# Gate and up products of two token chunks in seven block products for eight, with the last chunk in a pass of its own

## The chip, the cores and the metric

The kernel runs on one core of one Trainium2 chip. The metric is the device time of one execution in microseconds. A core has a matrix engine (TensorE, PE in the rows), VectorE (DVE), ScalarE (ACT), GpSimd (POOL) and SyncE (SP, which here issues all DMAs). Matmuls write to banks in PSUM; tiles lie in SBUF, weights and results in the chip's memory.

## The reference, cut to what matters

One layer of a hybrid encoder: a modulated RMSNorm, one input projection, eight stick-breaking and eight forgetting attention heads, an output projection, and a SwiGLU feed-forward, for 1024 prompt tokens and 64 sample tokens. D_MODEL is 1024, D_FF is 2816, everything is float32. What the change touches:

```python
x = x + (1.0 + ada[2]) * (o @ w_o)
h = rmsnorm(x, g_ffn) * (1.0 + ada[4]) + ada[3]
f = (jax.nn.silu(h @ w_gate) * (h @ w_up)) @ w_down
x = x + (1.0 + ada[5]) * f
y = rmsnorm(x, g_final)
```

## The kernel before, in words

Activations lie transposed, features on the 128 partitions and tokens along the columns. The 1088 tokens form three chunks (`CH`, line 29) of 384, 384 and 320 columns; the last holds 256 prompt tokens and the 64 sample tokens, so each of its modulated steps is two instructions (`pieces`, line 157). D_MODEL is eight tiles of 128 (`KT`), D_FF twenty-two blocks of 128 (`NFF`).

Every dense product keeps float32 accuracy through two parts: an operand is rounded to a high part (`hi`, a ScalarE copy, line 173) and the rest is its low part (`lo`, a subtraction of two SBUF tensors, line 176). A product is then three matmuls per k tile, high by high, low by high and high by low (`dense`, lines 422 to 429).

After attention, `out_block` (line 850) multiplies with `w_o`; `evac_plain` (line 1019) adds to the residual `x1`, `square1` (line 1047) sums the squares, and `norm2(c)` (line 1061) makes the feed-forward's input of chunk c: column sums and a reciprocal root (`token_cols`, `rstd_cols`, lines 187 to 215), spread over all partitions by small matmuls (`spread`, line 217), then a scale (line 1086), a shift with rounding to the high part `h2h` (line 1090) and the low part `h2l` (line 1091) for each of eight tiles.

The feed-forward (lines 1160 to 1228) runs over eleven groups of two D_FF blocks. `load_ff` (line 1165) loads a block's columns of `w_gate` and `w_up`, 512 KB each, and splits them, the low part on VectorE. `hidden` (line 1177) makes, for one block and one chunk, the gate and up products of 24 matmuls each in banks tagged `z`, then silu on ScalarE, the multiply by the up product, the rounding to `dh` and the low part `dl`. Then the group's two `w_down` blocks are loaded and split, and for each chunk and each of eight output tiles m six matmuls are summed in one of three banks (`t`, `t`, `acc`, line 1212) and VectorE adds the result to `x1` (line 1222). In the last group `weigh` (line 1127) also sums squares for the final norm, and `final(c)` (line 1139) transposes chunk c, scales and stores it.

The order of the instructions is a planner's: it takes them by priority and simulated time, per engine, so work whose operands are ready passes work that waits. Each engine then runs its own list strictly in order. Tiles of one tag rotate through a fixed number of buffers, and a DMA into a tile waits for the last reader of the buffer's former tile.

## Time and profile before

| | us |
|---|---|
| median of three runs (1682.41 to 1685.65) | 1683.74 |
| profiled execution | 1681.39 |
| its span, first to last instruction | 1679.2 |
| TensorE busy in the span | 1580.3 (94%) |
| one feed-forward group, 1045.36 to 1116.81 | 71.45 |

How to read the rows below: a stretch of time is given in us from the span's start. Busy time of an engine is the time in which it ran at least one instruction; behind it stands the number of instructions. "[2.24 <-DVE x L1022]" behind an instruction is the engine's idle time before it and the instruction that ended it. A number after L is a line of the kernel. Neighbouring instructions of one engine overlap a little, so starts are better than durations for a pace.

### The profile page before, as it was taken

Reading aid. Unit: us, or ns where it says so; the run is one execution under the profiler, and the core shown is the slowest. Engines: PE = TensorE matmul, PEld = TensorE weight load, DVE = VectorE, ACT = ScalarE, POOL = GpSimd, SP = SyncE. Lnnn points to the kernel's source line nnn. Section 1 sums busy time; section 2 is a strip of 40 time slices with the busy share of each in tenths; the row PEclk is TensorE's granted clock in tenths of the full one; section 3 lists DMA queues with packets and bytes.
Section 4 is the critical chain, followed back from the end, with each engine's and each line's share of the span. In section 5 each row is a group of like instructions: output and inputs, shape, how many; then the busy total and the mean of one; then the engine's idle time right before and its main releaser. Section 6 shows DMA issues by size and latency. Waiting matters only on the chain.

```text
span 1679.2 us, 26182 instructions
## 1 busy us (share of the span) xinstructions
PE 1580.3 (94%) x9822; PEld 1487.7 (89%) x9822; DVE 947.0 (56%) x1828; ACT 657.1 (39%) x1410; POOL 604.9 (36%) x556
## 2 busy tenths in 40 slices
PE   8898998988899977998999999999999999999998
PEld 4697887867888966987989999999999999999997
DVE  5659767598557565676895334334443344334336
ACT  5466656577445553555454021120211112021127
POOL 2558778797668774773360000000000000000004
PEclk9999999999999987999999999999999999999999
DMA  9433333321444552463332021110202102021002
GB/s 309 165 102 93 110 92 100 93 78 32 125 121 121 151 144 63 114 184 100 91 101 63 2 76 39 38 51 26 76 15 62 51 26 71 6 76 50 27 26 107
DMA packets 174750, 141.61 MB, mean 84 GB/s; under 512 B 14336, under 2 KB 167584, under 8 KB 174624
## 3 DMA queue, kind: packets, MB, share of 16 engines
q1 hardware_dynamic: 174624, 139.94, 28.8%
q8 instruction: 78, 1.28, 0.3%
q14 instruction: 48, 0.39, 0.1%
HBM read 105.60 MB, written 27.08 MB: 79 GB/s over the span
## 4 chain that ended last, share of the span: by engine, by line
PE 65%; DVE 4%; POOL 2%; DMA 1%; ACT 1%; issue 1%; SPq 1%; DVEq 0%; POOLq 0%; ACTq 0%
PE gu L428 10%; PE gu L429 10%; PE gu L427 10%; PE acc_d L1219 5%; PE acc_d L1217 5%; PE acc_d L1218 5%; PE acc L427 2%; PE acc L428 2%; PE acc L429 2%; PE ps_av L756 2%; PE pt_a L747 2%; PE acc_o L427 2%; PE acc_o L428 1%; PE acc_o L429 1%; PE ps_z L691 1%
## 5 line engine op out<-in xcount | busy, mean ns | idle before, releaser
L428 PE MATMUL gu<-h,wff_l 128*128 128x384 f32 (+1 forms) x1056 | 345.3, 327 | 0.0
L429 PE MATMUL gu<-h,wff_h 128*128 128x384 f32 (+1 forms) x1056 | 345.1, 327 | 0.0
L427 PE MATMUL gu<-h,wff_h 128*128 128x384 f32 (+1 forms) x1056 | 343.5, 327 | 0.0
L1222 DVE SCALAR_TENSOR_TENSOR x<-acc_d,ada,x 128x384 f32<-128x384 f32 (+1 forms) x352 | 167.0, 498 | 251.2 <-PE acc_d L1219 251.1
L1135 POOL TENSOR_TENSOR sums<-sums,sq 128x384 f32<-128x384 f32 (+1 forms) x17 | 16.8, 990 | 774.7 <-ACT sq L1134 770.8
L427 PE MATMUL acc<-h,whi 128*128 128x384 f32 (+1 forms) x576 | 199.5, 346 | 5.7 <-DVE kraw L500 3.2
L428 PEld LDWEIGHTS gu<-h,wff_l 128*128 128x128 f32 x1056 | 198.2, 188 | 0.0
L429 PEld LDWEIGHTS gu<-h,wff_h 128*128 128x128 f32 x1056 | 198.2, 188 | 0.0
L427 PEld LDWEIGHTS gu<-h,wff_h 128*128 128x128 f32 x1056 | 198.0, 188 | 0.0
L429 PE MATMUL acc<-h,whi 128*128 128x384 f32 (+1 forms) x576 | 193.3, 336 | 3.7 <-DVE h L404 3.7
L428 PE MATMUL acc<-h,wlo 128*128 128x384 f32 (+1 forms) x576 | 193.5, 336 | 0.0
L1217 PE MATMUL acc_d<-dh,wdh 128*128 128x384 f32 (+1 forms) x528 | 173.5, 329 | 0.1
L1219 PE MATMUL acc_d<-dl,wdh 128*128 128x384 f32 (+1 forms) x528 | 172.9, 328 | 0.0
L1218 PE MATMUL acc_d<-dh,wdl 128*128 128x384 f32 (+1 forms) x528 | 172.8, 327 | 0.0
L711 DVE TENSOR_TENSOR_SCAN kp<-kp 128x384 f32<-128x384 f32 (+4 forms) x104 | 140.1, 1354 | 37.5 <-ACT kp L707 35.5
L1184 ACT ACTIVATE sg<-gu 128x384 f32<-128x384 f32 (+1 forms) x66 | 31.3, 474 | 279.2 <-PE gu L429 279.2
L1186 ACT CAST dh<-sg 128x384 fp32r<-128x384 f32 (+1 forms) x66 | 32.5, 493 | 269.6 <-DVE sg L1185 269.6
L747 PE MATMUL pt_a<-ident,a_t 128*128 128x128 f32 x608 | 103.9, 283 | 30.3 <-DVE aT L753 17.0
L441 ACT CAST aT<-pt_a 128x384 fp32r<-128x384 f32 (+3 forms) x208 | 98.9, 481 | 82.0 <-PE pt_a L747 70.7
L753 DVE TENSOR_TENSOR aT<-pt_a,aT 128x384 fp32r<-128x384 f32 (+3 forms) x208 | 110.0, 535 | 36.4 <-ACT aT L441 35.5
L715 POOL TENSOR_TENSOR a_t<-a_t,kp 128x383 f32<-128x383 f32 (+6 forms) x104 | 114.1, 1105 | 31.7 <-DVE kp L711 10.3
L427 PEld LDWEIGHTS acc<-h,whi 128*128 128x128 f32 x576 | 111.4, 193 | 10.9 <-DVE kraw L500 3.6
(307 smaller groups left out, 3334.0 us busy)
## 6 DMA issues: line engine op xcount, KB each, us to landing
lowraw<-in_w_ada SPq DMA_DIRECT2D x32, 512.0 KB, 3.5
wraw<-in_w_in SPq DMA_DIRECT2D x24, 512.0 KB, 6.4
wraw<-in_w_gate SPq DMA_DIRECT2D x22, 512.0 KB
wraw<-in_w_up SPq DMA_DIRECT2D x22, 512.0 KB, 3.7
wraw_d<-in_w_down SPq DMA_DIRECT2D x22, 512.0 KB, 3.5
wa<-in_w_ada SPq DMA_DIRECT2D x16, 512.0 KB, 6.7
oT_d<-ot SPq DMA_DIRECT2D x128, 64.0 KB, 2.1
wraw<-in_w_o SPq DMA_DIRECT2D x14, 512.0 KB, 3.3
```

What stands on the lines that cost most here:

```text
L427: pe.matmul(out=acc, lhsT=wh[:, kt, :], rhs=rh[kt], start=st, stop=False)
L428: pe.matmul(out=acc, lhsT=wl[:, kt, :], rhs=rh[kt], start=False, stop=False)
L429: pe.matmul(out=acc, lhsT=wh[:, kt, :], rhs=rl[kt], start=False, stop=sp_)
L441: act.copy(out=out, in_=in_)
L711: dve.tensor_tensor_scan(out=rev, data0=rev, data1=rev, initial=1.0 if b == w else kp[:, b:b + 1], op0=ALU.mult, op1=ALU.min)
L715: eng[E_AM[qt]].tensor_tensor(out=a_t[:, :wm], in0=a_t[:, :wm], in1=kp[:, a + 1:a + 1 + wm], op=ALU.mult)
L747: pe.transpose(out=pt[:, j * P:(j + 1) * P], in_=at[a][:, j * P:(j + 1) * P], identity=ident)
L753: dve.tensor_tensor(out=tl, in0=pv, in1=f32(th), op=ALU.subtract)
L1217: pe.matmul(out=a_, lhsT=wh[:, m, :], rhs=dh[:, t0:t0 + n], start=(i == 0), stop=False)
L1218: pe.matmul(out=a_, lhsT=wl[:, m, :], rhs=dh[:, t0:t0 + n], start=False, stop=False)
L1219: pe.matmul(out=a_, lhsT=wh[:, m, :], rhs=dl[:, t0:t0 + n], start=False, stop=(i == G - 1))
L1222: dve.scalar_tensor_tensor(out=xc[:, a:b], in0=acc[:, a:b], scalar=ada[:, 5, m, s:s + 1], in1=xc[:, a:b], op0=ALU.mult, op1=ALU.add)
```

## The change

The eight input tiles k of a gate or up product, two D_FF blocks and the first two chunks form two by two blocks each. Seven products of sums of blocks replace the eight block products (Strassen's scheme in Winograd's form). The weight sums (`Seven`) are four GpSimd instructions on 512 columns for each matrix and group, and each of the seven weight operands is split by `prep`, the low part on VectorE. The activation operands are seven sets of four tile pairs, made once by `norm2_steps` in pieces between the work of pass 1. `Blocks` multiplies: twelve matmuls a product, accumulated in three banks, with copies and adds between them.

The last chunk can't be paired, so it gets a pass of its own over all 22 blocks ahead of the others (pass 1, the loop over `f0`), with all weights loaded and split once for it and once more for chunks 0 and 1 (pass 2, the loop over `g0`). In pass 1, three of six low parts of a group are GpSimd's; in pass 2, that of `wd[0]`. The weight tiles rotate through four raw buffers and three pairs of parts. Inside the feed-forward the planner is switched off for TensorE, ScalarE, VectorE and GpSimd (`manual_schedule`): they run in the order of the program. The norms of chunks 0 and 1 (`rms_rows`) come in the first down loop of pass 1. `down_begin` starts three blocks with one of the two D_FF blocks before the other is needed. The final norm of the last chunk moves into the first group of pass 2, that of chunk 1 among the last down blocks; chunk 0 ends the kernel.

The core of the diff; chunk 1 is c = 1, and `later(left)` issues the low parts that were put off:

```diff
-    def norm2(c):
+    def rms_rows(c, out=None):
+
         n = CH[c][1]
...
+        def part_tiles():
+
+            i = count["w"] % 3
+            count["w"] += 1
+            return tuple((wpool if i < 2 else fp).tile([P, KT, P], F32R, tag=t, name=t) for t in ("whi", "wlo"))
...
+        def part(src, hi, lo, lo_eng=dve):
+            act.copy(out=hi, in_=src)
+            lo_eng.tensor_tensor(out=lo, in0=src, in1=f32(hi), op=ALU.subtract)
+            return hi, lo
...
+        def down_begin(wd, dd, c, ahead=1):
+
+            for m in range(3):
+                begun[m] = bank(("t", "t", "acc")[m % 3], "acc_d")
+                down_products(begun[m], wd, dd, c, m, ahead, True)
+
+        def down_block(wd, dd, c, m, last, ahead=1):
+
+            n = CH[c][1]
+            if m in begun:
+                acc = begun.pop(m)
+            else:
+                acc = bank(("t", "t", "acc")[m % 3], "acc_d")
+                down_products(acc, wd, dd, c, m, ahead, True)
+            down_products(acc, wd, dd, c, m, 1 - ahead, False)
...
+            if last:
+                weigh(m, c, xc, n)
...
+                for kt, c, w in ((k, 0, "11"), (k, 1, "12"), (4 + k, 1, "22"), (4 + k, 0, "21")):
+                    def scale(kt=kt, c=c, w=w, b=b):
+                        t = b[w] = opl.tile([P, 384], F32, tag=("xn2", "sq")[c], name=f"n{w}")
+                        dve.scalar_tensor_tensor(
+                            out=t, in0=x1[kt][c], scalar=sc2[:, kt, 0:1], in1=sacc[c], op0=ALU.mult, op1=ALU.mult)
...
+                    def diff(out=out, x_=x_, y_=y_, b=b):
+                        pool.tensor_tensor(out=b[out], in0=b[x_], in1=b[y_], op=ALU.subtract)
...
+                    def low(out=out, k=k, w=w, b=b):
+                        dve.tensor_tensor(out=bh[w, k, 1], in0=b[out], in1=f32(bh[w, k, 0]), op=ALU.subtract)
+                    chains.append((diff, high, low))
...
+            for i in range(len(chains) + 2):
+                yield [chains[i - j][j] for j in (2, 1, 0) if 0 <= i - j < len(chains)]
...
-        G = 2
-        for g0 in range(0, NFF, G):
...
+        def half_tile():
+            if spare:
+                return spare.pop()
+            t = part_tiles()
+            spare.append([x_[:, 4:8] for x_ in t])
+            return [x_[:, 0:4] for x_ in t]
+
+        class Seven:
+
+            def __init__(self, f0, w):
+                r1, r2 = (raw_tile(col_src(w, f0 + i)) for i in range(2))
+                self.a11, self.a12, self.a21, self.a22 = r1[:, 0:4], r1[:, 4:8], r2[:, 0:4], r2[:, 4:8]
+                self.ops = []
+
+            def sums_first(self):
+                self.s1 = fp.tile([P, 4, P], F32, tag="s1", name="s1")
+                pool.tensor_tensor(out=self.s1, in0=self.a21, in1=self.a22, op=ALU.add)
+                pool.tensor_tensor(out=self.a21, in0=self.a11, in1=self.a21, op=ALU.subtract)
+
+            def sum2(self):
+                pool.tensor_tensor(out=self.a11, in0=self.s1, in1=self.a11, op=ALU.subtract)
+
+            def sum4(self):
+                pool.tensor_tensor(out=self.a12, in0=self.a12, in1=self.a11, op=ALU.subtract)
+
+            def prep(self):
+                src = (self.a11, self.a12, self.a11, self.s1, self.a21, self.a12, self.a22)[len(self.ops)]
+                self.ops.append(part(src, *half_tile()))
...
+        BAND = ("11", "21", "T2", "T1", "T3", "22", "T4")
...
+            def product(self, i):
...
+                acc = getattr(self, "zxzvzvz"[i])
+                wh, wl = self.s.ops[i]
+                for k in range(4):
+                    for j, (w_, r_) in enumerate(((wh, 0), (wl, 0), (wh, 1))):
+                        pe.matmul(
+                            out=acc, lhsT=w_[:, k, :], rhs=bh[BAND[i], k, r_],
+                            start=(i in (0, 1, 3) and k == 0 and j == 0),
+                            stop=(k == 3 and j == 2), skip_group_check=True)
+
+            def evac(self, i):
+                if i == 0:
+                    self.m1 = gu_tile("m1")
+                    act.copy(out=self.m1, in_=self.z)
+                elif i == 1:
+                    dve.tensor_tensor(out=self.m1, in0=self.m1, in1=self.x, op=ALU.add)
+                    self.done(0, 0, self.m1, self.m1)
+                elif i == 2:
+                    self.u2 = gu_tile("u2")
+                    act.copy(out=self.u2, in_=self.z)
+                elif i == 3:
+                    self.m5 = gu_tile("m5")
+                    act.copy(out=self.m5, in_=self.v)
+                elif i == 4:
+                    dve.tensor_tensor(out=self.m5, in0=self.m5, in1=self.z, op=ALU.add)
+                    self.done(1, 1, self.m5, self.m5)
+                elif i == 5:
+                    dve.tensor_tensor(out=self.u2, in0=self.u2, in1=self.v, op=ALU.add)
+                    self.done(0, 1, self.u2, self.u2)
+                else:
+                    self.done(1, 0, self.z, None)
+
+        ET = mybir.EngineType
+        in_order = tc.manual_schedule(engines={ET.PE, ET.Activation, ET.DVE, ET.Pool})
...
+        def ready(*key, lo_eng=dve):
+            parts[key] = part(raws.pop(key), *part_tiles(), lo_eng)
...
+        def gated(ff, gu):
+            sg = sgs.pop(ff)
+            dve.tensor_tensor(out=sg, in0=sg, in1=gu[:, :n2], op=ALU.mult)
+            dh, dl = (gu_tile("d", F32R)[:, 0:n2] for _ in range(2))
+            dds[ff % 2, 2] = dh, dl
+            act.copy(out=dh, in_=sg)
+            left.append(lambda: dve.tensor_tensor(out=dl, in0=sg, in1=f32(dh), op=ALU.subtract))
+
+        silu(0, gate_up("g", 0))
+        for g, f0 in enumerate(groups):
+            last = f0 + 2 == NFF
+            f1 = f0 + 1
+
+            gu = gate_up("u", f0)
+            ready("u", f1, lo_eng=pool)
+            fetch("d", f0)
+            gated(f0, gu)
+            gu = gate_up("g", f1)
+            later(left)
+            if g > 0:
+                step2()
+            fetch("d", f1)
+            if last:
...
+            else:
+                fetch("g", f0 + 2)
+                ready("g", f0 + 2)
+            silu(f1, gu)
+            if g > 0:
+                step2()
+            gu = gate_up("u", f1)
+            ready("d", f0, lo_eng=pool)
+            gated(f1, gu)
+            later(left)
...
+            else:
+                gu = gate_up("g", f0 + 2)
+                ready("d", f1)
+                silu(f0 + 2, gu)
+                fetch("u", f0 + 2)
+                fetch("g", f0 + 3)
+            wd = [parts.pop(("d", f0)), parts.pop(("d", f1))]
+            dd = {(i, 2): dds.pop((i, 2)) for i in range(2)}
+            if g > 0:
+                step2()
+            down_begin(wd, dd, 2, 0)
+            for m in range(KT):
+                down_block(wd, dd, 2, m, last, 0)
+                if m == 0 and not last:
+                    ready("u", f0 + 2, lo_eng=pool)
+                if g > 0 and m == 6:
+                    step2()
...
+                if g == 0 and m in (2, 5):
+                    rms_rows(m // 3, sacc[m // 3])
+            if not last:
+                fetch("u", f0 + 3)
+                ready("g", f0 + 3)
...
+        cur7 = first7
+        for gi, g0 in enumerate(groups):
...
+            def up(i, c, src, out):
+                s_ = sg[i, c]
+                dve.tensor_tensor(out=s_, in0=s_, in1=src, op=ALU.mult)
+                dh, dl = (hb.tile([P, 384], F32R, tag="dd", bufs=8, name="d") for _ in range(2))
+                act.copy(out=dh, in_=s_)
+                left.append(lambda: dve.tensor_tensor(out=dl, in0=s_, in1=f32(dh), op=ALU.subtract))
+                dd[i, c] = dh, dl
...
+            else:
+                B = Blocks(cur7, ("z", "z", "z"), gate)
+            for i in range(7):
+                if gi or i > 1:
+                    B.product(i)
+                if i == 0 and gi:
+                    cur7.prep()
+                    cur7.prep()
+                elif i == 1:
+                    cur7.prep()
+                    cur7.prep()
+                    up7 = Seven(g0, w_up)
+                elif i == 2:
+                    cur7.prep()
+                    up7.sums_first()
+                    up7.prep()
+                    up7.sum2()
+                    raws["d", 1] = raw_tile(down_src(g0 + 1))
+                elif i == 4:
+                    up7.prep()
+                    up7.sum4()
+                    up7.prep()
+                    raws["d", 0] = raw_tile(down_src(g0))
+                elif i == 6:
+                    up7.prep()
+                    up7.prep()
+                if gi or i > 0:
+                    B.evac(i)
+            B = Blocks(up7, ("av", "z", "u"), up)
+            for i in range(7):
+                B.product(i)
+                later(left)
...
+                if i == 1:
+                    up7.prep()
+                    up7.prep()
+                    if not last:
+                        nx7 = Seven(g0 + 2, w_gate)
+                elif i == 3:
+                    wd = [None, part(raws.pop(("d", 1)), *part_tiles())]
+                    if not last:
+                        nx7.sums_first()
+                elif i == 5:
+                    wd[0] = part(raws.pop(("d", 0)), *part_tiles(), pool)
+                B.evac(i)
+            down_begin(wd, dd, 1)
+            later(left)
+            for bi, (c, m) in enumerate([(c, m) for c in (1, 0) for m in range(KT)]):
+                down_block(wd, dd, c, m, last)
+                if not last:
+                    if bi in (1, 2):
+                        nx7.prep()
+                    elif bi == 3:
+                        nx7.sum2()
+                        nx7.sum4()
+                elif c == 0 and m == 2:
+                    col1 = final_cols(1)
+                elif c == 0 and m in (4, 5, 6):
+                    final_tile(col1, 1, m - 4)
+                if gi == 0 and c == 1:
+                    if m in (3, 5, 7):
+                        final_last(col2, m // 2 - 1)
+            if not last:
+                cur7 = nx7
+        in_order.__exit__(None, None, None)
+        col0 = final_cols(0)
+        for j in range(3):
+            final_tile(col0, 0, j)
```

## Rows read from the trace of the kernel before

**Rows 1.** Busy time of the engines over the span, the page's first part:
```profile
PE 1580.3 (94%) x9822; PEld 1487.7 (89%) x9822; DVE 947.0 (56%) x1828; ACT 657.1 (39%) x1410; POOL 604.9 (36%) x556
```

**Rows 2.** Stretches: length, busy PE, PEld, DVE, ACT, POOL (instructions), granted clock, DMA share, GB/s:
```profile
845.00:862.00 17.00, 13.99 (x78) 13.25 (x78) 16.50 (x33) 10.00 (x23) 12.66 (x9) 1.00 0.34 105
862.00:876.00 14.00, 14.00 (x82) 14.00 (x81) 11.54 (x19) 7.32 (x14) 9.32 (x7) 0.88 0.27 77
876.00:930.00 54.00, 54.00 (x325) 53.79 (x324) 32.15 (x60) 23.68 (x38) 1.57 (x1) 1.00 0.23 69
...
1188.26:1616.94 428.68, 428.68 (x2593) 428.68 (x2593) 170.90 (x301) 70.93 (x109) 0.00 (x0) 1.00 0.15 45
```

**Rows 3.** Timeline of TensorE in one group: start us, duration us, engine, line, instruction:
```profile
1045.03 0.33 PE L429 MATMUL gu<-h,wff_h 128*128 128x384 f32 x1
...
1057.68 0.31 PE L427 MATMUL gu<-h,wff_h 128*128 128x320 f32 x1
...
1063.84 0.31 PE L427 MATMUL gu<-h,wff_h 128*128 128x320 f32 x1
```

**Rows 4.** DMA issues: tile, queue, count, KB each, median us from issue to landing:
```profile
wraw<-in_w_in SPq DMA_DIRECT2D x24, 512.0 KB, 6.4
...
wraw<-in_w_up SPq DMA_DIRECT2D x22, 512.0 KB, 3.7
wraw_d<-in_w_down SPq DMA_DIRECT2D x22, 512.0 KB, 3.5
```

**Rows 5.** VectorE by line and shape from 840 us on: count, busy us, mean ns, idle:
```profile
L1222 DVE SCALAR_TENSOR_TENSOR x<-acc_d,ada,x 128x384 f32<-128x384 f32 x176 | 107.5, 617 | 168.5 <-PE acc_d L1219 168.5
L176 DVE TENSOR_TENSOR wff_l<-wraw,wff_h 128x1024 fp32r<-128x1024 f32 x44 | 54.3, 1235 | 53.1 <-ACT wff_h L173 52.3 <-issue 0.8
L1222 DVE SCALAR_TENSOR_TENSOR x<-acc_d,ada,x 128x256 f32<-128x256 f32 x88 | 42.5, 483 | 82.7 <-PE acc_d L1219 82.6
...
L1187 DVE TENSOR_TENSOR dl<-sg,dh 128x384 fp32r<-128x384 f32 x44 | 24.4, 555 | 14.5 <-ACT dh L1186 14.5
L1222 DVE SCALAR_TENSOR_TENSOR x<-acc_d,ada,x 128x64 f32<-128x64 f32 x88 | 24.2, 275 | 0.0
```

**Rows 6.** ScalarE by line and shape from 840 us on, columns as in rows 5:
```profile
L173 ACT CAST wff_h<-wraw 128x1024 fp32r<-128x1024 f32 x44 | 45.9, 1044 | 39.9 <-PE gu L429 37.6 <-DMA wraw<-in_w_up 1.4 <-DMA wraw<-in_w_gate 0.9
...
L1186 ACT CAST dh<-sg 128x384 fp32r<-128x384 f32 x44 | 22.6, 513 | 264.8 <-DVE sg L1185 264.8
```

**Rows 7.** GpSimd by line and shape over the whole span, columns as in rows 5:
```profile
L176 POOL TENSOR_TENSOR wlo<-wraw,whi 128x1024 fp32r<-128x1024 f32 x26 | 64.1, 2465 | 27.2 <-ACT whi L173 22.0 <-PE pt_xr L353 4.7 <-POOL wlo L176 0.4
...
L1135 POOL TENSOR_TENSOR sums<-sums,sq 128x384 f32<-128x384 f32 x14 | 14.2, 1014 | 769.6 <-ACT sq L1134 768.8
```

**Rows 8.** Timelines near 846 and 852 us, and line 1091's durations (min/median/max ns):
```profile
846.00 2.42 POOL L176 TENSOR_TENSOR wlo<-wraw,whi 128x1024 fp32r<-128x1024 f32 x1
847.26 2.79 DVE L1091 SCALAR_TENSOR_TENSOR h<-xn,ada,h 128x256 fp32r<-128x256 f32 x3
...
852.31 2.40 POOL L176 TENSOR_TENSOR wlo<-wraw,whi 128x1024 fp32r<-128x1024 f32 x1
852.36 0.60 DVE L1022 SCALAR_TENSOR_TENSOR x<-acc_o,ada,x 128x384 f32<-128x384 f32 x1
...
L1091 DVE SCALAR_TENSOR_TENSOR h<-xn,ada,h x32: 270/614/2464, 847.3 to 902.7; 128x384 fp32r<-128x384 f32 x16, 128x256 fp32r<-128x256 f32 x8, 128x64 fp32r<-128x64 f32 x8
```

**Rows 9.** Timeline of TensorE near 861 us, idle time before the instruction in brackets:
```profile
861.26 0.44 PE L427 MATMUL acc_o<-fo_qs,whi 128*128 128x384 f32 x1 [2.24 <-DVE x L1022]
```

**Rows 10.** Timelines of VectorE, ScalarE and TensorE at the end, columns as in rows 3:
```profile
1651.46 0.16 DVE L213 TENSOR_SCALAR col<-pc 128x3 f32<-128x3 f32 x1 [0.16 <-PE pc L202]
1652.09 1.28 ACT L189 ACT_TABLE_LOAD   x1
1655.21 0.89 DVE L194 TENSOR_TENSOR col<-col 128x3 f32<-128x3 f32 x1
...
1666.50 0.31 PE L1219 MATMUL acc_d<-dl,wdh 128*128 128x320 f32 x1
```

More of the change, by code (lines that the diff above doesn't have):

```diff
@@ L71 @@
 FP = (2, -1, 0, 0)
+HBW = 3
+NPG = (1, 3, 5, 7)
 QT = (6, 7, 0, 1, 4, 5, 2, 3, 8)
@@ L1141, in final, with step2, final_cols @@
+        steps2 = norm2_steps()
+        def step2():
+            for f in next(steps2, ()):
+                f()
+        def final_cols(c):
             col = opl.tile([P, 2, 3], F32, tag="col", name="col3")
             token_cols([sums[c]], chunk_toks(c), D, col, "u")
[L1143 to L1158 removed]
```

283 lines of the change are left out of this document (174 added, 109 removed).

## The prediction, made before the changed kernel was run

> **What bounds the kernel now.** I read the page's busy shares first, then a table by stretch, then TensorE's own timeline. TensorE is busy 94% of the span [rows 1]. In the table [rows 2] the feed-forward is perfectly regular: from 1188.26 to 1616.94 us TensorE has no idle time at full granted clock (1.00, the 2.4 GHz level), while VectorE works 171 of 429 us, ScalarE 71 and GpSimd none. So this stage is a stream of matmuls and nothing else, and its time is a count times a pace. The pace is in the timeline [rows 3]: 73 matmuls of 384 columns between 1045.03 and 1057.68 give 173.3 ns each, 42 of 320 columns between 1057.68 and 1063.84 give 146.7 ns. (The 0.33 us beside each is a latency; neighbours overlap.) One group of two feed-forward blocks holds 432 matmuls, 288 wide and 144 narrow, hence 49.9 + 21.1 = 71.0 us, as the table's 428.68 us for six groups (71.45 each) confirms.
>
> **Part 1, seven products for eight.** Per weight matrix and group, two blocks by two chunks by eight k tiles by three parts were 96 matmuls; seven products of four k tiles by three are 84. Two matrices and eleven groups save 264 matmuls of 384 columns: 264 x 0.1733 = 45.8 us, all of it on the path. The last chunk's matmuls and all of the down projection keep their count and width. Pass 1 is 144 x 0.1467 = 21.1 us a group, pass 2 264 x 0.1733 = 45.8 us a group (2.08 a product, 16.6 for down).
> The Trainium skill (TensorE: Matmul & The Clock Gate, Back-to-back issue gap) states N / 2.4 + 2.5 ns for this gap when warm. By that the saving would be an estimated 42.9 us; the trace's 173.3 ns is longer, and decides.
>
> **Part 2, weights loaded twice.** The last chunk has its own pass, so 66 more loads of 512 KB. Pass 1 wants six in 21.1 us, 149 GB/s. I cost it at nothing: the stretch 845 to 862 moved 105 GB/s at a DMA share of 0.34 [rows 2], so 149 would be about half. A load lands 3.5 to 3.7 us after issue [rows 4]. In pass 1 the tightest is the next gate tile: its slot is free about 2 us into a group, it lands at 5.8, is split by 8.2 (1.05 on ScalarE, 1.24 on VectorE, below) and is read at 10.6. If a load took 6.4 us as those of w_in do [rows 4], it would be read 0.3 us late, 3 us over the pass.
>
> **Part 3, the splitting and summing work.** ScalarE and VectorE take 1.05 and 1.24 us for 1024 columns [rows 5, 6], GpSimd 2.47 [rows 7]. By the same rows and those of 384 columns I estimate a half tile of 512 at 0.6 on ScalarE, 0.7 on VectorE and 1.3 on GpSimd. GpSimd, idle here before, gets three low parts a group in pass 1 (7.4 us) and the halves of the norm's differences, and in pass 2 eight sums (10.4) and one low part (2.5). By totals everything fits. VectorE's pass 1: three low parts 3.7, four gating steps 2, eight evacuations 6.1, the norm's steps 3, some 15 of 21.1 us; pass 2: fourteen half low parts 9.8, one whole 1.2, fourteen steps on 384 columns at 0.56 7.8, sixteen evacuations at 0.62 9.9, some 29 of 45.8 [rows 5].
> But the totals miss one thing. At 846.00 GpSimd runs a low part for 2.42 us, and VectorE's three L1091 pieces, begun at 847.26, take 2.79 us; the same line takes 270 ns at least, 2464 at most [rows 8]. Its operands are both in SBUF. The evacuation L1022, with one operand in PSUM, runs in its usual 0.60 us at 852.36 under an equal GpSimd instruction [rows 8]. So a VectorE instruction with two SBUF operands stands still until the GpSimd instruction ends, and all behind it on VectorE's queue stand too. What that does to TensorE is there as well: at 861.26 it had idled 2.24 us for an evacuation that had stood behind such pieces [rows 9].
> The Trainium skill (SBUF — State Buffer, Who interferes with whom) has the rule: GpSimd shares its ports with VectorE, and a VectorE instruction with two SBUF inputs contends with one of GpSimd that reads SBUF. The trace agrees (2464 against 270 ns). Without the rule the sum would be that of the first rival.
>
> **Part 4, program order.** Four engines now run in the written order, so a late VectorE instruction holds the evacuations behind it, and TensorE cannot take up other work meanwhile: it has three banks for the down blocks, so a block waits where the evacuation of the third before it is late. I walked one group of each pass with these durations.
> Pass 1: VectorE's evacuations (0.48 + 0.28 us a block [rows 5], against 0.88 of TensorE) start about when their blocks end; the low part of wd for f1 is ready 0.5 to 1.5 us ahead, that of the next gate tile 0.3 to 0.8 us. I take 0.3 us a group, 3 us (0 to 11, the upper end one 1.0 us GpSimd difference [rows 7] in front of it each time).
> Pass 2, gate half: GpSimd's sums delay two splits; the copy of the first bank ends near the 8.3 us at which product 4 needs it. 0.2 us a group, 2 us (0 to 9).
> Pass 2, end of the up half, in us from its start: the next gate's raw tiles land at 8.5 (slots freed by the last two splits at 4.6, then 3.7 [rows 4]); their two sums, after VectorE's low part of wd[1], end at 11.7. The multiply of (1,1), both operands in SBUF, waits for that: 12.2; its copy on ScalarE 12.7 [rows 6]; behind it ScalarE's copy of wd[0], 13.7; then GpSimd's low part of wd[0], after one VectorE multiply, 14.15 to 16.6. TensorE ends product 6 at 14.6, does nine matmuls with wd[1] and wants that low part at 16.3. The low part of d(0,1) stands until 16.6 and ends at 17.1: TensorE 0.7 us late. Behind it on VectorE come the multiply and low part of (1,0), to 18.6, and only then the first evacuation, 19.2 [rows 5], where the fourth block wants its bank at 18.4: 0.85 more. Some 1.6 us a group, 17 us. Bounds: nothing (GpSimd ends early) and one whole low part, 2.4 us a group, 26 us [rows 7]. I take the walk, as the 2.24 of [rows 9] is that mechanism.
>
> **Part 5, single costs.** The two rms_rows stand in the written order inside the first down loop: TensorE's matmuls of the spread wait for column sum, square root and five small VectorE steps. Before, such a chain ran from 1651.46 to the end of L194 at 1656.1, an activation table load of 1.28 in it, with other work on TensorE meanwhile [rows 10]. Here nothing else can pass: about 3 us for the first and 2 for the second, 5 us (3 to 9, with GpSimd's low part of u in front of the small steps, or a granted clock that falls, as to 0.88 of 862 to 876, part of it at the 1.2 GHz level, after 3.0 us of idle time in the stretch before [rows 2]: 0.12 x 14 = 1.7 us). First weights and the change from pass 1 to pass 2, where the low part of wd stands behind four sums on GpSimd: 1 us (0 to 3). The last chunk's outputs share the down loop's banks, 1 us; the tail, 12.4 us from the last matmul's end to the span's end [rows 10], gets a third full output tile for a half one, and three banks for six: 2.5 us. Together 3.5 (0 to 7). What norm2 of chunks 0 and 1 leaves behind before the stage is worth nothing: TensorE is busy all of 876 to 930, where those ran [rows 2].
>
> **The sum** is -45.8 + 3 + 2 + 17 + 5 + 1 + 3.5 = -14.3 us on the profiled execution (1681.4; its span is 1679.2), so 1667. The median of the runs lies 2.3 above that execution, and the changed kernel will be told by its median: **1669 us**.
>
> **Rivals.** (a) The locks hide: the GpSimd instructions fall where VectorE runs evacuations or nothing, and the passes cost at most 6 us. For it: VectorE needs only 29 of 45.8 us, and a delay in one product has until the next but one to heal. Against: the written order puts wd[0]'s low part just where down begins. Then -45.8 + 6 + 9.5 = -30, 1653 us; with nothing lost in the passes 1647.
> (b) Slower: the lock on SBUF decides everything. If one GpSimd low part stands in front of the path in each of the 22 group passes, at 2.4 us, 53 us come back: -45.8 + 53 + 9.5 = +17, 1700 us. It makes the change a loss when the passes lose over 36 us, 1.65 a group pass. For it: the 2.24 in [rows 9], and an order that no scheduler mends. Against: in pass 1 my walk leaves slack in each group.
> (c) Loads too slow for pass 1: 3 us, or 1672; a load that is late every time by the difference of 6.4 and 3.7 us would still cost under 30 us.
>
> **How the numbers follow.** The forecast's own case, passes losing 12 to 33 us, is 1660 to 1681 and has 0.45. Rival (a), 1644 to 1660, has 0.30, with (c) inside these two. The rest, 0.25, is beyond 1681: 0.10 for a time within 0.2% (about 3.4 us, what a measurement of this kernel can tell from no change) of 1683.7, and 0.15 for (b). Faster thus 0.75, same 0.10, slower 0.15. The range of eight in ten leaves out the foot of (a) and the far half of (b): 1646 to 1688.
>
> **What would show it.** TensorE's matmul count falls by 264, and the pace stays 173.3 and 146.7 ns. The step of part 4 is right if TensorE's idle time in pass 2 has VectorE's dl and evacuation as its releasers near the start of each down loop, 1 to 2 us a group, with VectorE rows of 2 us and more beside GpSimd's; wrong if a group of pass 2 lasts 45.8 us. A group of pass 1 should last 21 to 22 us, with no idle time put down to a DMA. The first down loop should show two gaps of 2 to 4 us before the spread. The prediction falls if the pace of the new matmuls differs, if pass 1 loses over 1 us a group, or if the raw tiles land late.

## The result, and the profile after

The changed kernel takes 1706.01 us (median of four runs, 1705.14 to 1708.5), the kernel before 1683.08 beside it: ratio 1.0138, 95% interval 1.012 to 1.0155. It is 23 us slower where 14 us faster was forecast, and outside the range of 1646 to 1688.

The busy times, for the first line [rows 1]:

```profile
PE 1561.3 (92%) x9558; PEld 1449.6 (85%) x9558; DVE 1129.8 (66%) x2042; ACT 808.6 (47%) x1687; POOL 850.6 (50%) x703
```

The 264 matmuls are gone (9822 to 9558). What came back is seen by stage. Stretches of the changed kernel (columns as in [rows 2]): first group with the norms; groups 2 to 10 of pass 1; the last group of pass 1 with the first of pass 2; groups 2 to 10 of pass 2; the last group and the end. The last line is the kernel before, from its first feed-forward matmul on:

```profile
874.99:911.24 36.25, 30.34 (x194) 29.17 (x194) 17.25 (x38) 13.90 (x21) 11.70 (x6) 0.95 0.50 146
911.24:1103.23 191.99, 191.99 (x1298) 190.06 (x1297) 127.46 (x251) 91.01 (x136) 83.39 (x43) 1.00 0.50 149
1103.23:1190.49 87.26, 74.32 (x417) 70.94 (x415) 49.02 (x84) 34.42 (x64) 31.05 (x22) 0.94 0.27 76
1190.49:1634.35 443.86, 425.43 (x2378) 414.23 (x2377) 289.05 (x405) 147.05 (x272) 123.43 (x81) 1.00 0.22 65
1634.35:1704.80 70.45, 57.37 (x325) 54.84 (x324) 38.14 (x66) 37.51 (x69) 18.64 (x15) 0.91 0.16 61
```
```profile
871.75:1679.20 807.45, 799.65 (x4862) 797.41 (x4861) 340.31 (x625) 171.44 (x280) 19.43 (x19) 1.00 0.16 48
```

From each length I take its matmuls at the old pace (173.3 ns wide, 146.7 narrow). The first stretch has 168 narrow ones, 24.6 us; the second 1296 narrow, 190.1; the third 120 narrow and 264 wide, 63.4; the fourth 2376 wide, 411.8; the last 264 wide, 45.8. Lost beyond them: 11.6, 1.9, 23.9, 32.1 and 24.7, together 94.2 us. The kernel before lost 26.1 of its 807.45 (781.4 of matmuls). So 68.1 us more are lost, 45.8 saved, and the stage began 3.2 later: 25.6, the difference of the spans (1704.8 and 1679.2).

Pass 1 is as good as a stream can be: a group lasts 21.33 us for 21.12 of matmuls, at 149 GB/s. Pass 2 lasts 49.32 a group for 45.76. One such group begins at 1338.49; its gate and up products take 29.25 us (168 matmuls, 29.1 by the pace), its 96 down matmuls 20.30 for 16.64. The loss stands at their start. GpSimd, then VectorE, ScalarE and TensorE there (columns as in [rows 3] and [rows 9]):

```profile
1362.98 1.29 POOL L1320 TENSOR_TENSOR s<-wraw 128x512 f32<-128x512 f32 x1 [11.95 <-DMA wraw<-in_w_gate]
1364.34 1.29 POOL L1321 TENSOR_TENSOR wraw<-wraw 128x512 f32<-128x512 f32 x1
1367.63 2.39 POOL L1167 TENSOR_TENSOR wlo<-wraw,whi 128x1024 fp32r<-128x1024 f32 x1 [1.99 <-ACT whi L1166]
1374.97 1.30 POOL L1324 TENSOR_TENSOR wraw<-s,wraw 128x512 f32<-128x512 f32 x1 [4.95 <-DVE wlo L1167]
...
1363.83 0.55 DVE L1371 TENSOR_TENSOR m<-m,gu 128x384 f32<-128x384 f32 x1 [1.61 <-PE gu L1352]
1364.42 1.63 DVE L1506 TENSOR_TENSOR m<-m,m 128x384 f32<-128x384 f32 x1
...
1367.69 2.74 DVE L1506 TENSOR_TENSOR u<-u,u 128x384 f32<-128x384 f32 x1
1371.01 0.56 DVE L1509 TENSOR_TENSOR d<-u,d 128x384 fp32r<-128x384 f32 x1 [0.58 <-ACT d L1508]
...
1373.09 1.14 DVE L1202 SCALAR_TENSOR_TENSOR x<-acc_d,ada,x 128x384 f32<-128x384 f32 x2
...
1375.27 1.55 DVE L1167 TENSOR_TENSOR wlo<-wraw,whi 128x512 fp32r<-128x512 f32 x1
...
1366.50 1.05 ACT L1166 CAST whi<-wraw 128x1024 fp32r<-128x1024 f32 x1
1370.46 0.51 ACT L1508 CAST d<-u 128x384 fp32r<-128x384 f32 x1 [2.91 <-DVE u L1506]
...
1371.03 0.44 PE L1179 MATMUL acc_d<-d,whi 128*128 128x384 f32 x1 [1.54 <-ACT d L1508]
1371.31 0.34 PE L1180 MATMUL acc_d<-d,wlo 128*128 128x384 f32 x1
...
1373.75 0.44 PE L1179 MATMUL acc_d<-d,whi 128*128 128x384 f32 x1 [0.65 <-DVE x L1202]
...
1377.40 0.44 PE L1179 MATMUL acc_d<-d,whi 128*128 128x384 f32 x1 [0.23 <-DVE x L1202]
```

The two multiplies of L1506 with two SBUF operands take 1.63 and 2.74 us where the third form of the line, with one operand in PSUM, takes 0.55. Each ends 0.4 us after a GpSimd instruction that had begun ahead of it: the first after L1321 (ahead by 0.08 us), the second after the low part of wd[0] (by 0.06 us). ScalarE's copy, TensorE's d(0,1) and the first evacuation (1373.09) follow. A third lock stands in the down loop: a split's low part takes 1.55 us at 1375.27 beside GpSimd's next sum, where the split before it took 0.68, and the evacuation behind it is what TensorE waits for at 1377.40. The evacuations L1202 run at their 0.6 us. The Trainium skill (SBUF — State Buffer, Who interferes with whom) adds to the rule of the prediction that the order of issue decides who blocks; the 0.06 us here and the runs below agree. Durations of L1506 over the kernel (min/median/max ns):

```profile
L1506 DVE TENSOR_TENSOR m<-m,m x22: 557/558/1641, 1155.8 to 1660.3; 128x384 f32<-128x384 f32 x22
L1506 DVE TENSOR_TENSOR u<-u,u x11: 2310/2731/2752, 1164.5 to 1662.5; 128x384 f32<-128x384 f32 x11
```

The first multiply is not locked in every group. In seven of groups 2 to 10 L1321 began ahead of it: it takes 1.39 to 1.64 us and the group 49.3 to 49.7. In the other two the multiply began first: it takes 0.88 and 0.56 us and the group 48.8 and 48.5. So one kernel, without any edit, shows what this lock is worth: 0.5 to 1.2 us of the group.

The norms and the change of passes, TensorE's waits first, then GpSimd's low part of wd for f0, and a split in the down loop on ScalarE and VectorE with the evacuation behind it:

```profile
901.45 0.91 PE L223 MATMUL bc<-ident,col 128*128 128x128 f32 x6 [1.89 <-DVE col L196]
907.17 1.48 PE L223 MATMUL bc<-ident,col 128*128 128x128 f32 x6 [1.60 <-DVE col L196]
1120.48 0.41 PE L1180 MATMUL acc_d<-d,wlo 128*128 128x320 f32 x1 [2.22 <-POOL wlo L1167]
1127.10 0.39 PE L1179 MATMUL acc_d<-d,whi 128*128 128x320 f32 x1 [1.88 <-DVE x L1202]
1130.02 0.60 PE L1179 MATMUL acc_d<-d,whi 128*128 128x320 f32 x1 [1.79 <-DVE x L1202]
1141.81 0.44 PE L1352 MATMUL gu<-bT,whi 128*128 128x384 f32 x1 [2.91 <-ACT u L1366]
...
1117.11 3.32 POOL L1167 TENSOR_TENSOR wlo<-wraw,whi 128x1024 fp32r<-128x1024 f32 x1
...
1125.04 0.60 ACT L1166 CAST whi<-wraw 128x512 fp32r<-128x512 f32 x1
...
1125.67 0.69 DVE L1167 TENSOR_TENSOR wlo<-wraw,whi 128x512 fp32r<-128x512 f32 x1 [2.01 <-ACT whi L1166]
1126.28 0.67 DVE L1202 SCALAR_TENSOR_TENSOR x<-acc_d,ada,x 128x256 f32<-128x256 f32 x2
```

VectorE waits 2.01 us at 1125.67 for a split that stands on ScalarE behind the final norm's square and scale of the last block (`weigh`), and the next evacuation stands behind it: one block's evacuation, square, scale and split in series, against 0.88 us of matmuls.

### The profile page after: what moved, and what is told of

Read it like the earlier page. It is cut to its first block, busy times and chain, and to the rows that moved or that the text cites. A ratio compares the mean times of both kernels' runs of the same rounds, so it can differ in the third digit from the quotient of the medians.

```text
span 1704.8 us, 26702 instructions
## 1 busy us (share of the span) xinstructions
PE 1561.3 (92%) x9558; PEld 1449.6 (85%) x9558; DVE 1129.8 (66%) x2042; ACT 808.6 (47%) x1687; POOL 850.6 (50%) x703
## 5 line engine op out<-in xcount | busy, mean ns | idle before, releaser
L1166 ACT CAST whi<-wraw 128x512 fp32r<-128x512 f32 (+1 forms) x220 | 168.5, 790 | 198.6 <-PE acc_d L1181 163.1
L1167 DVE TENSOR_TENSOR wlo<-wraw,whi 128x512 fp32r<-128x512 f32 (+1 forms) x177 | 169.5, 974 | 93.6 <-ACT whi L1166 87.9
L1202 DVE SCALAR_TENSOR_TENSOR x<-acc_d,ada,x 128x256 f32<-128x256 f32 (+1 forms) x352 | 163.1, 496 | 81.4 <-PE acc_d L1181 80.1
L1179 PE MATMUL acc_d<-d,whi 128*128 128x384 f32 (+1 forms) x528 | 180.5, 342 | 25.2 <-ACT d L1508 12.5
L1352 PE MATMUL gu<-bT,whi 128*128 128x384 f32 x704 | 188.6, 339 | 2.9 <-ACT u L1366 2.9
L1167 POOL TENSOR_TENSOR wlo<-wraw,whi 128x1024 fp32r<-128x1024 f32 x43 | 106.4, 2475 | 164.7 <-ACT whi L1166 158.0
L1180 PE MATMUL acc_d<-d,wlo 128*128 128x384 f32 (+1 forms) x528 | 175.2, 332 | 2.2 <-POOL wlo L1167 2.2
L1181 PE MATMUL acc_d<-d,whi 128*128 128x384 f32 (+1 forms) x528 | 176.5, 334 | 0.0
L1352 PEld LDWEIGHTS gu<-bT,whi 128*128 128x128 f32 x704 | 129.6, 190 | 3.4 <-ACT u L1366 3.2
L717 POOL TENSOR_TENSOR a_t<-a_t,kp 128x383 f32<-128x383 f32 (+6 forms) x104 | 112.9, 1094 | 33.5 <-DVE kp L713 10.5
L429 PEld LDWEIGHTS acc<-h,whi 128*128 128x128 f32 x576 | 111.4, 193 | 11.0 <-DVE kraw L502 3.6
L1352 PE MATMUL gu<-bT,wlo 128*128 128x384 f32 x352 | 119.0, 338 | 0.0
L431 PEld LDWEIGHTS acc<-h,whi 128*128 128x128 f32 x576 | 111.5, 194 | 5.2 <-DVE h L406 4.8
```

Source lines behind the costliest of these rows:

```text
L429: pe.matmul(out=acc, lhsT=wh[:, kt, :], rhs=rh[kt], start=st, stop=False)
L431: pe.matmul(out=acc, lhsT=wh[:, kt, :], rhs=rl[kt], start=False, stop=sp_)
L717: eng[E_AM[qt]].tensor_tensor(out=a_t[:, :wm], in0=a_t[:, :wm], in1=kp[:, a + 1:a + 1 + wm], op=ALU.mult)
L1166: act.copy(out=hi, in_=src)
L1167: lo_eng.tensor_tensor(out=lo, in0=src, in1=f32(hi), op=ALU.subtract)
L1179: pe.matmul(out=a_, lhsT=wh[:, m, :], rhs=dh, start=first, stop=False)
```

## The experiments

Unless said, a kernel is the changed one with the edit. For pass 2 the number compared is the length of groups 2 to 10 divided by nine, since identical code ahead of the stage let it begin anywhere from 871.0 to 878.4 us in these profiled executions, which puts up to 7 us into a single time. The three joint kernels ran four times each, all others once.

**Engine of one low part (a1_low_vector).**
```diff
-                    wd[0] = part(raws.pop(("d", 0)), *part_tiles(), pool)
+                    wd[0] = part(raws.pop(("d", 0)), *part_tiles(), dve)
```


> One edit to the changed kernel: in pass 2 the low part of wd[0] is VectorE's, not GpSimd's, at the same place of the order. A pass-2 group of the changed kernel lasts 49.3 us, 3.6 above the 45.76 of its matmuls. Lock theory: the loss is the multiply of (0,1) standing for 2.74 us under GpSimd's low part; it falls to 0.56, 2.2 us a group come back, the group lasts about 47.1 and the kernel 1682 to 1686. Order theory: VectorE's own queue is what is late; the low part (1.24 us) now stands in it ahead of the add and the multiply, which end 0 to 0.5 us earlier than before; the group lasts 48.8 to 49.3 and the kernel 1700 to 1706.


Measured: 1700.65 us. The stretch of nine groups, and L1506:
```profile
1192.41:1630.12 437.71, 424.32 (x2377) 412.70 (x2377) 280.65 (x414) 147.05 (x272) 102.01 (x72) 1.00 0.23 66
```
```profile
L1506 DVE TENSOR_TENSOR u<-u,u x11: 557/558/561, 1166.6 to 1659.9; 128x384 f32<-128x384 f32 x11
```
The multiply of (0,1) is free (558 ns), yet the group lasts 48.63: 0.7 us back, not 2.2. That is near the order theory's 48.8 to 49.3, but the mean is of two kinds of group. In three of the nine the multiply of (1,1) began ahead of GpSimd's L1321 and took 0.56 to 0.69 us; these groups last 47.9 to 48.0. In six it took 1.51 to 1.67 us, and they last 48.9 to 49.0. So the other lock still costs 1.0 us in most groups. What keeps the free groups 0.8 us above the 47.1 of the lock theory is not shown: VectorE now does the low part itself, in front of the add and the multiply, and the split in the down loop still takes 1.53 us.

**First two sums off the up half (a2_sums_later).**
```diff
-                    if not last:
-                        nx7.sums_first()
...
                     elif bi == 3:
+                        nx7.sums_first()
                         nx7.sum2()
```


> One edit: the first two weight sums of the next group's gate matrix leave product 3 of the up half and stand with the other two in the down loop. GpSimd is then free when VectorE multiplies (1,1), which should fall from 1.63 to 0.56 us. Lock theory: everything behind it, ScalarE's copy of wd[0] and GpSimd's low part too, moves 1.1 us ahead, the group lasts about 48.2 and the kernel 1693 to 1697. Order theory: the same mechanism is worth less, since the add of (0,1) waits for product 5 anyway; 0 to 0.6 us a group, 1699 to 1706.


Measured: 1704.4 us, group 48.90 (440.11 / 9). The multiply of (1,1) is free (at most 559 ns), but that of (0,1) stands its full 2.75 us. Below it GpSimd, VectorE and TensorE in one group:
```profile
L1506 DVE TENSOR_TENSOR u<-u,u x11: 2745/2749/2754, 1165.4 to 1660.5; 128x384 f32<-128x384 f32 x11
```
```profile
1320.50 1.59 POOL L1320 TENSOR_TENSOR s<-wraw 128x512 f32<-128x512 f32 x1
...
1321.53 0.97 DVE L1509 TENSOR_TENSOR d<-u,d 128x384 fp32r<-128x384 f32 x1 [0.58 <-ACT d L1508]
...
1321.55 0.44 PE L1179 MATMUL acc_d<-d,whi 128*128 128x384 f32 x1 [0.47 <-ACT d L1508]
1322.56 0.44 PE L1181 MATMUL acc_d<-d,whi 128*128 128x384 f32 x1 [0.39 <-DVE d L1509]
```
All did move ahead: TensorE waits 0.47 us for the high part of d(0,1) where it waited 1.54. But GpSimd starts the moved sums as soon as its low part ends, the low part of d(0,1) now takes 0.97 us beside them, and TensorE waits 0.39 us for it. Only 0.4 us a group comes back. The size is the order theory's; in the rows a lock that was taken away comes back in another place.

**Both, and the split a product earlier (a3_early).**
```diff
-                elif i == 5:
-                    wd[0] = part(raws.pop(("d", 0)), *part_tiles(), pool)
+                elif i == 4:
+                    s0, (h0, l0) = raws.pop(("d", 0)), part_tiles()
+                    act.copy(out=h0, in_=s0)
                 B.evac(i)
+                if i == 4:
+                    dve.tensor_tensor(out=l0, in0=s0, in1=f32(h0), op=ALU.subtract)
+                    wd[0] = h0, l0
```


> The edit of a2, and wd[0] split one product earlier with its low part on VectorE behind the multiply of (1,1), so that GpSimd runs nothing in the up half. Walk with the measured durations: low part of d(0,1) ready 0.4 us before TensorE wants it, first evacuation 0.2 us late: the group lasts 46.0 to 46.6 and the kernel 1674 to 1680, faster than the kernel before. Order theory gives the same, as both the lock and the place are gone. A theory in which the loss comes from something else (the banks, the loads, the pace of the matmuls) leaves the group above 48.5.


Measured: 1687.6 us, group 47.78 (430.02 / 9), short of the 46.0 to 46.6. GpSimd and VectorE in one group:
```profile
1307.52 1.30 POOL L1320 TENSOR_TENSOR s<-wraw 128x512 f32<-128x512 f32 x1 [11.84 <-DMA wraw<-in_w_gate]
1308.89 1.29 POOL L1321 TENSOR_TENSOR wraw<-wraw 128x512 f32<-128x512 f32 x1
...
1309.07 1.53 DVE L1506 TENSOR_TENSOR m<-m,m 128x384 f32<-128x384 f32 x1
```
The sums were moved into the down loop, but nothing waits on GpSimd ahead of them any more, so they start when their tiles land, in the up half, and lock the multiply of (1,1) as before. The program's place of an instruction sets only its order on its own engine.

**No GpSimd in the up half (a5_no_gpsimd).** On top of a3:
```diff
-                    elif bi == 3:
-                        nx7.sums_first()
-                        nx7.sum2()
-                        nx7.sum4()
+                    elif bi in (4, 6, 8):
+                        (nx7.sums_first, nx7.sum2, nx7.sum4)[bi // 2 - 2](dve)
```


> The edit of a3_early, and the four weight sums of the next gate matrix on VectorE in the down loop. In a3_early GpSimd still ran the first two of them in the up half (they start when the tiles land, wherever the program has them), the multiply of (1,1) stood 1.53 us, and a pass-2 group lasted 47.8. Lock theory: the multiply falls to 0.56, the queue behind it moves 1.0 ahead, the group lasts 46.7 to 47.0 and the kernel 1677 to 1680. Rival, VectorE as the bound: its 2.8 us of sums delay the evacuations of the down loop, the group stays at 47.5 or above and the kernel at 1685 or above.


Measured: 1674.9 us in one run (the kernel before beside it 1683.29 to 1686.16), and a group of 46.77:
```profile
1184.32:1605.22 420.90, 418.73 (x2377) 413.51 (x2377) 283.63 (x450) 147.97 (x272) 55.01 (x36) 1.00 0.24 68
```
The multiply of (1,1) takes at most 559 ns, and 1.0 us came back, though VectorE has more work (450 instructions for 405). Its amount of work is not the bound. With the multiply's lock that of the split in the down loop went too (0.68 us for 1.53); this run does not part the two.

**A GpSimd instruction that nobody waits for (d1_unread).** On top of a5:
```diff
+                    for k in (0, 4):
+                        pool.tensor_tensor(
+                            out=idle, in0=f32(h0[:, k:k + 3, :]), in1=f32(h0[:, k:k + 3, :]), op=ALU.add)
```


> The kernel of a5_no_gpsimd, whose pass-2 group lasts 46.77 us and in which GpSimd runs nothing in the up half, plus two GpSimd additions of 384 columns (about 1.0 us each) that read the high part of wd[0] when ScalarE has made it and write a tile that nobody reads. No instruction waits for them. Lock theory: they start as VectorE begins the low part of wd[0] (two SBUF operands, 1.22 us), which or whose followers stand until they end; VectorE's queue moves back 1.0 to 2.0 us, the group lasts 47.6 to 48.8 and the kernel 1683 to 1695. No lock, order and dependences alone: the group stays at 46.8 and the kernel at 1673 to 1677.


Measured: 1683.19 us, 8.3 above a5; group 47.43 (426.90 / 9), 0.67 above, just under the 0.8 to 2.0 of the lock theory and far from the 0 of the other. VectorE and GpSimd in one group:
```profile
1307.20 1.22 DVE L1562 TENSOR_TENSOR wlo<-wraw,whi 128x1024 fp32r<-128x1024 f32 x1
1308.34 1.18 DVE L1510 TENSOR_TENSOR d<-m,d 128x384 fp32r<-128x384 f32 x1
...
1307.24 2.97 POOL L1565 TENSOR_TENSOR idle<-whi 128x384 f32<-128x384 f32 x2 [13.93 <-ACT whi L1559]
```
This is the cleanest test: no instruction waits for the additions, and the tile that they read comes free no later for them, since TensorE reads it through the down loop that begins at 1310.05. Yet VectorE's next subtraction takes 1.18 us for 0.55. The size was off because VectorE issued first, by 0.04 us: its low part ran at 1.22, and GpSimd stood (2.97 us for two additions that take 1.02 each alone). Each engine locked the other out in turn.

**The early split on GpSimd (e1_early_gpsimd).** As a3's diff, with `pool` for `dve`, and the sums left where they were.


> The changed kernel with one edit: ScalarE's copy of wd[0] one product earlier, ahead of its copy of d(1,1), and the low part still GpSimd's. With GpSimd late the group lasts 49.3, with VectorE late (a1) 48.9, with VectorE early (a3) 47.8. Place theory: what matters is that ScalarE's copy no longer waits for the locked multiply of (1,1); the engine is worth what it was worth late, 0.4, so the group lasts 48.0 to 48.4 and the kernel 1692 to 1697. Lock theory: GpSimd now works without a break from the sums to the end of that low part, and VectorE's low part and multiply stand under it as long as before; 48.8 to 49.3, 1700 to 1706.


Measured: 1704.09 us, group 48.80 (439.17 / 9), at the edge of the lock theory's range and 0.4 outside the other's. What stands now is another instruction of the same queue, the low part of d(1,1):
```profile
1319.85 2.10 DVE L1509 TENSOR_TENSOR d<-m,d 128x384 fp32r<-128x384 f32 x1 [0.58 <-ACT d L1508]
...
1318.81 2.72 POOL L1563 TENSOR_TENSOR wlo<-wraw,whi 128x1024 fp32r<-128x1024 f32 x1
```

**The planner's order (a4_planner).** Only `manual_schedule` is taken out.


> The four engines' order is the planner's again, everything else as in the changed kernel. Order theory: TensorE may pass work that waits, the two gaps at the norm rows (8 us), the change of passes (24 us) and the end close up; 1660 to 1680. Lock theory: the planner doesn't know the lock, so the passes keep 2 to 3.5 us a group and only the single gaps close; 1685 to 1700. If the written order is better than the planner's, it is above 1710.


Measured: 1720.02 us, the third case. Nine groups of pass 2 (1219.25 to 1661.58) take 49.15 us each, no better than in written order; groups of pass 1 take 22.28 (one begins its gate product at 1026.58, the next at 1048.86) for 21.33. So the planner's order does not get the time back either. The run changes the order of four engines everywhere, so it does not say what a better order is worth; the joint kernels below try one.

**The norms (b1_spread_later).**
```diff
-                if g == 0 and m in (2, 5):
-                    rms_rows(m // 3, sacc[m // 3])
+                if g == 0 and m in (0, 2):
+                    cols.append(opl.tile([P, 2, 9], F32, tag="col", name="col2"))
+                    token_cols([sacc[m // 2]], chunk_toks(m // 2), D, cols[-1])
+                if g == 0 and m in (5, 7):
...
+                    spread(bc, cols[c], chunk_toks(c))
```


> The changed kernel with one edit in pass 1: column sums of the two norms after down blocks 0 and 2, their spread matmuls only after blocks 5 and 7, so that TensorE works while the column chain runs. The two gaps with their slow stretch cost 8.0 us of TensorE's time (15.0 for the 48 matmuls of the first down loop, clean 7.0). If TensorE's wait for the chain is the cause, the down loop lasts 9 to 11 us and the kernel 1700 to 1702; if VectorE's queue, with the chain ahead of the evacuations, is the cause, it stays at 13 and above and the kernel above 1703.


Measured: 1707.25 us in all, with a stage that began 3.4 later than the changed kernel's. The first down loop, here and in the changed kernel:
```profile
899.00:910.18 11.18, 10.31 (x74) 9.64 (x73) 7.25 (x28) 3.55 (x6) 2.40 (x1) 1.00 0.39 121
```
```profile
896.21:911.24 15.03, 11.54 (x74) 11.42 (x73) 6.34 (x26) 4.22 (x8) 2.41 (x1) 0.89 0.32 94
```
3.9 us back, to the edge of the 9 to 11 foreseen, and the granted clock stays 1.00 instead of 0.89: half of the 8.0 was TensorE's wait for the chain, with the clock that fell behind it. The total misses the 1700 to 1702, most of it by the late start: from the stage's first matmul on this kernel takes 827.1 us, the changed one 829.8.

**The change of passes (b2_change).** wd for f0 split on VectorE, the four sums behind it, two splits of the next weights after down blocks 3 and 5 instead of 1 and 2, and:
```diff
-            if last:
+            if last and c == 2:
+                weighs.append(lambda: weigh(m, c, xc, n))
+            elif last:
                 weigh(m, c, xc, n)
```


> The changed kernel with edits at the change of passes alone: the squares and weights of the last chunk's final norm are put off from the last down loop of pass 1 to the gate products of pass 2, wd for f0 is split on VectorE and GpSimd's four sums stand behind it. The stretch from the last pass-1 group to the second pass-2 group lasts 87.3 us, 24 above its matmuls. If the chain evacuation, ScalarE square and scale, ScalarE split, VectorE low part, next evacuation is the cause, the down loop falls from 15.4 us to 8 to 10 and 10 to 14 us come back: 1692 to 1696. If it is the amount of work on ScalarE and VectorE, the loss moves into the gate products: 1702 and above.


Measured: 1696.88 us. The whole stretch, and the down loop in it:
```profile
1101.84:1183.22 81.38, 72.41 (x417) 69.73 (x415) 48.73 (x85) 33.81 (x64) 29.58 (x21) 0.96 0.28 82
1116.57:1123.83 7.26, 7.26 (x50) 7.05 (x49) 5.17 (x15) 1.34 (x3) 1.14 (x2) 1.00 0.26 74
```
The down loop falls from 15.39 to 7.26, so its loss lay in what these edits moved: the chain through ScalarE (the waits of 1.88 and 1.79 us for an evacuation) and GpSimd's late low part (2.22 us). The run does not part the two. 5.9 us of the whole stretch come back, and 2.3 move into the products that follow, where the put-off squares stand before a bank copy (a wait of 2.41 us) and the column sums of the last chunk's norm make another of 2.44. Both theories hold in part.

**All together (c1_all, c2_all, c3_all).** c1 joins a5, b1, b2 and three edits: the multiply and low part of (1,0) after the first down blocks, the square-root table loaded ahead of the last down loop, all sums of squares on GpSimd.


> All of a5_no_gpsimd, b1_spread_later and b2_change, the multiply and low part of (1,0), which the first eight down blocks don't need, behind the first down blocks, and at the end the square-root table loaded ahead and all sums of squares on GpSimd. If the losses are separate waits with their own causes, the gains add: group 45.9 to 46.5 (31 us), 4 to 6, 10 to 14 and 3, together 1651 to 1658. If they share a cause, VectorE's queue being simply too full, most of the sum is missing: 1668 to 1685.


Measured: 1676.63 us, ratio 0.995 (0.993 to 0.9969): the sum missed by 20 and the group 47.67, in the range of the theory that VectorE's queue is simply too full. c2, whose VectorE does the same in another order, speaks against that; it corrects what c1's waits named:
```diff
-                    if bi in (1, 2):
+                    if bi in (4, 6):
                         nx7.prep()
-                    elif bi in (4, 6, 8):
-                        (nx7.sums_first, nx7.sum2, nx7.sum4)[bi // 2 - 2](dve)
+                    elif bi in (8, 10, 12):
+                        (nx7.sums_first, nx7.sum2, nx7.sum4)[bi // 2 - 4](dve)
```


> The joint kernel again. In c1_all the group was 47.67, not the hoped 46.0: with the multiply of (1,0) moved behind the first down block, the two splits for the next gate stood with it ahead of the evacuations (waits of 0.33 and 0.61 us on them). Here these splits stand after down blocks 4 and 6, the sums after 8, 10 and 12. The last chunk's squares start two products later, so that the bank copy that kept TensorE waiting 2.41 us is not behind them, and its column sums wait for the first down blocks (3.16 us of waiting before). If these waits are the causes, the group lasts 45.9 to 46.5, the change of passes 4 to 6 us less than the 81.3 of c1_all, and the kernel 1656 to 1662. If VectorE's amount of work is the limit, 1670 and above.

> As c2_all, but with the multiply and low part of (1,0) ahead of the first down blocks as in a5_no_gpsimd. If this pair in front of the first evacuation is what a5_no_gpsimd's groups still lose (0.9 us), the group lasts 46.5 to 46.8 and the kernel is 4 to 8 us above c2_all; if not, the two agree within 2 us.


Measured: c2 1655.12 us (four runs, 1654.52 to 1660.57), ratio 0.984 (0.9817 to 0.9863), 1.6% faster than the kernel before; c3 1657.53, 0.9845 (0.983 to 0.986). In c2 the change of passes and nine groups of pass 2:
```profile
1097.93:1173.88 75.95, 69.64 (x417) 66.62 (x415) 48.30 (x90) 33.93 (x64) 21.72 (x16) 1.00 0.30 87
1173.88:1588.96 415.08, 415.08 (x2378) 414.14 (x2377) 282.55 (x450) 147.93 (x272) 55.00 (x36) 1.00 0.24 69
```
A group lasts 46.12 us (c3: 46.32), 0.4 above its matmuls. That c3 lies 4 to 8 us above c2 was wrong (it lies 2.4 above, inside the spread of c2's runs): the pair (1,0) is worth 0.2 us a group, and 0.45 of a5's last 1.0 was the splits and sums early in the down loop (c3 against a5). c2's change of passes still holds 12.6 us beyond its matmuls.

## Why the prediction was wrong, point by point

- **Part 1** holds: 264 matmuls fewer, pace 173.3 and 146.7 ns, 45.8 us saved.
- **Part 2** holds: pass 1 ran at 149 GB/s and DMA share 0.50, as said, with TensorE busy all 191.99 us from 911.24 on. Rival (c) falls. Pass 2 is another matter: the walk had the next gate's raw tiles landed 8.5 us into the up half, but GpSimd's first sum, which waits for them, began at 9.6 to 10.5 us in groups 2 to 10. That late raw tiles would be a sign against the prediction stood in it. They did not put GpSimd's low part ahead of the multiply of (0,1): in a2, where both sums are out of the up half, it still stands 2.75 us, and the two groups of the changed kernel with the latest tiles (10.0 and 10.5 us) are its two short ones.
- **Part 3**, the lock, is the mechanism, and d1 shows it with no new wait between instructions. VectorE's evacuations, with an operand in PSUM, kept their 0.6 us beside it. The 270 and 2464 ns of the prediction are of one line with pieces of different widths; like with like, a multiply of 384 columns took 558 ns free and 2731 locked. The lock stood in pass 1 as well (the low part of `d`, L1423, took 493 to 1795 ns there), but TensorE waited for nothing behind it.
- **Part 4, pass 1** and the **gate half**: 0.2 us a group for 0.3, and 0.1 for both halves' products where 0.2 was set for the gate half.
- **Part 4, end of the up half, is the step that failed**, a size: 1.6 us a group forecast, 3.4 measured (3.56 a group, less 0.13 in the products), outside the bound of 2.4 too. The walk let the multiply of (0,1) go ahead of GpSimd's low part; it came 0.06 us too late and stood under nearly all of it (2310 to 2752 ns in all eleven groups), so d(0,1)'s high part was late, where the walk had only its low part late, by 0.7 us. The wait of the multiply of (1,1) was in the walk, but the upper bound counted one low part alone: two locks in one queue add, and the third, of a split in the down loop, was in neither. Over eleven groups that is some 39 us for the 19 in the sum, gate half included. This alone took the forecast's gain: it is 20 of the 39.5 us between the forecast and the profiled execution (1667 and 1706.6); the second failure below is 18.
- **Part 5, norms**: 8.0 for 5, inside its 3 to 9. The two gaps are there, a little under the 2 to 4 us foreseen (1.89 and 1.60).
- **Part 5, first weights and change of passes** is the second failure: 1 us (0 to 3) forecast. The first weights cost 3.6 (21.22 us from 874.99 to the first down matmul, 17.6 of matmuls). At the change the down loop lost 8.4 (15.39 less 7.04) and the first group's products 6.9 (31.81 us for 144 matmuls, 24.96). The prediction saw the low part behind four sums, 2.22 us of it, and missed that `weigh` stands on ScalarE ahead of the splits on which VectorE's queue hangs (b2).
- **Last chunk's outputs and tail**: the first pass-2 down loop, which holds these outputs, lost 8.7, 5.1 beyond the usual group; the last stretch 24.7, 21.1 beyond the group, where 12.4 + 2.5 was forecast.
- In the other direction, the 13.7 us that the kernel before lost in the stage outside its 12.4 us tail (26.1 in all) were silently kept in the sum; the losses above contain whatever is left of them.
- **Rival (b)** gave the sign and nearly the size (1700) for a loss of 1.65 us and more a group pass, but not its place: pass 1 lost nothing, pass 2 twice as much. **Rival (a)**, 1653 with the locks hidden, is close to what c2 measures, 1655, once GpSimd is out of the way; that the numbers meet is partly luck, since c2 also has the edits of b1 and b2. The chance of 0.15 for slower was too low: the walk turned on which of two instructions comes first, a matter of 0.06 us as measured, and its bounds didn't hold the other branch.

Not settled: how much of the single costs at the start, the change and the end is the lock and how much the order of ScalarE's and VectorE's queues; only b1, b2 and the joint kernels touched them, several edits at a time.

## What to carry to other kernels

Work given to an idle GpSimd is not free if VectorE, at that time, runs instructions with two SBUF operands that TensorE waits for: look for those instructions in the stretch, count every GpSimd instruction there, and assume that a race is lost (here leads of 0.02 to 0.15 us were enough, and groups of one kernel fell both ways). Moving a GpSimd instruction later in the program doesn't hold it back; give it an operand that comes late, or another engine. In a written order, keep what waits for another engine (a split, a column chain) out of the queue ahead of evacuations.

## What the runs showed of the hardware

- The lock works both ways: two GpSimd additions took 2.97 us where 1.02 each is their time alone, the first held by a VectorE low part that had begun 0.04 us earlier.
- A wait costs TensorE more than its length: the matmul after one is followed at 0.28 us instead of 0.17 (1371.03 to 1371.31, and as much after 1373.75 and 1377.40), some 0.1 us for each of these restarts.
- The down loop at the change of passes, with waits of 1.8 to 2.2 us, ran at a granted clock of 0.86, so part of it at the 1.2 GHz level: from 1130.42 on its narrow matmuls follow at 0.27 us instead of 0.15. The whole change of passes of c2 stayed at 1.00, the 2.4 GHz level. Columns as in [rows 2]:

```profile
1117.96:1133.35 15.39, 9.51 (x49) 8.54 (x49) 5.93 (x17) 7.27 (x16) 6.54 (x6) 0.86 0.24 70
```
